# Rounding a weight transfer's two halves with one instruction

## The chip, the cores and the metric

One core of a Trainium2 chip runs the program. The metric is device microseconds of one execution, as the median of several runs. The engines named below are PE (TensorE: the matmuls, with PEld for the loads of their stationary operand), ACT (ScalarE), DVE (VectorE), POOL (GpSimd) and SP (which issues the weight transfers).

## What is computed

Two blocks run on 256 tokens of width 1024 (plus 16 meta tokens in the first block). Cut to what matters here:

```
first block:   h = rms_norm(stream);  proj = h @ w_in
               y_a = layer_norm(depthwise_conv(a * sigmoid(gate))) -> silu -> @ conv_pw_out
               y_b = top-k sparse attention -> @ attn_w_o
               stream += (g_a * y_a + g_b * y_b) @ w_merge_out
               stream += (silu(a) * b_) @ ffn_down,   a, b_ = depthwise_conv(h @ ffn_up)
               out = rms_norm(stream)
second block:  layer 0: gated linear attention (GLA), layer 1: block attention (MoBA);
               after each:  x = layer_norm(alpha * x + y)
                            x = layer_norm(alpha * x + (silu(gate) * up) @ w_down)
```

All of it is float32, and each weight is used for all tokens once it has arrived.

## The kernel before

**How a product is made.** Each float32 factor is split into a high part (the value rounded to the type fp32r) and a rest (value minus high part, again fp32r), and a product is three matmuls: high times high, high times rest, rest times high. `mm_ws` (L173) has the weights as the stationary operand, `mm_xs` (L179) has them as the moving one. Activations are split by `split` (L199): an ACT copy for the high part, a DVE subtraction for the rest.

**How weights arrive.** The host packs all weights, in their order of use, into 167 chunks of 128 x 2048 (1 MB). `emit_raw` (L112) issues one transfer for each chunk from SP into a ring of three `wraw` tiles. A chunk is two halves of 1024 columns, and a half is the unit of use: `next_half` (L164) hands out the next one. In a projection (`proj_tile`, L188) a half is the stationary operand of 24 matmuls; in the down projections (L741) and in `xs_cols` (L868) it is the moving operand of 512 columns.

**How weights are split.** `emit_split` (L122) emits, for each half, an ACT copy into `whi` (L134) and a DVE subtraction into `wlo` (L136). Each of the two has a ring of LOOK + 1 = 6 tiles of 1024 columns. `may_split` (L144) sets how far ahead of use this goes: with half h about to be used, halves up to h + 5 are emitted. The tile of half h + 5 is that of half h - 1, so that its ACT copy waits until PE has finished the last matmul of half h - 1. `hold` (L156) puts a limit on this ahead of a normalization, `go_on` (L159) lifts it. Twelve "early" halves (L80) go to tiles of their own.

**What sets the order.** Each engine runs its instructions in one order that is fixed when the program is built. A planner makes it from the order in which the program emits them, their dependences and its own estimate of when each can start: an instruction that it holds to be ready goes ahead of an earlier one that isn't. Only inside `manual_schedule` blocks (the first normalization, L702, L772, `norms` L844) do DVE and ACT keep the order of the program.

**The stages, by the start of the span.** Convolution, index scores and sparse attention of the first block run until about 200 us, the merge until 274 us, the first feed-forward until 466 us, GLA until 586 us, the second feed-forward until 773 us, MoBA until 885 us, the third feed-forward until the end. A feed-forward (`ffn`, L710) goes through its 22 hidden tiles in groups of two: four halves of up projections (two for each hidden tile, with the results in `pa` and `pb`), then two halves of down projections. For each hidden tile `evac2` (L934; `evac1`, L756, in the first feed-forward) makes the activation `g_`, and `split` (L730) turns it into `rg_h` and `rg_l`, the stationary operands of the down projections. A group of four opens the second and third feed-forward, a group of six (TAIL) closes each.

Of the kernel before, what the change touches and what calls it, by code (L numbers as in the profile page):

```python
# [10 lines left out]
F32R = mybir.dt.float32r  # L11
# [5 lines left out]
P = 128  # L17
# [17 lines left out]
HALF = 1024  # L35
CHUNK = 2 * HALF
# [44 lines left out]
EARLY_SET = {e + i for e in EARLY for i in range(4)}  # L81
# [3 lines left out]
def tile_hybrid(ctx: ExitStack, tc: tile.TileContext, x, meta, wts, misc, vec, cst, rows, gkw, ng, pos,  # L85
# [5 lines left out]
    wp = ctx.enter_context(tc.tile_pool(name="wp", bufs=1))  # L91
# [14 lines left out]
    LOOK = LK  # L106
    RAW_BUFS = 3
    raws, halves = {}, {}
    state = {"raw": 0, "split": 0, "use": 0, "cap": 2 * N_CHUNKS, "early": None}
    early = []  # L110

    def emit_raw(upto):  # L112
        while state["raw"] < min(upto, N_CHUNKS):
            c = state["raw"]
            t = wp.tile([P, CHUNK], F32, name="wraw", tag="wraw", bufs=RAW_BUFS)
            for a in range(0, CHUNK, HALF if c == 0 else CHUNK):
                b = a + (HALF if c == 0 else CHUNK)
                nc.sync.dma_start(t[:, a:b], wts[c, :, a:b])
            raws[c] = t
            state["raw"] += 1  # L120

    def emit_split(upto, later=None):  # L122
        while state["split"] < min(upto, 2 * N_CHUNKS):
            h = state["split"]
            emit_raw(h // 2 + 1)
            r = raws[h // 2][:, (h % 2) * HALF:(h % 2 + 1) * HALF]
            if h in EARLY_SET:
                hi, lo = state["early"](len(early) % 4)
                early.append((hi, lo))
            else:  # L130
                hi = wp.tile([P, HALF], F32R, name="whi", tag="whi", bufs=LOOK + 1)
                lo = wp.tile([P, HALF], F32R, name="wlo", tag="wlo", bufs=LOOK + 1)
                halves[h] = (hi, lo)
            A.activation(hi, r, AF.Copy)  # L134
            if later is None:
                V.tensor_sub(lo, r, hi.bitcast(F32))  # L136
            else:
                later.append(lambda r=r, hi=hi, lo=lo: V.tensor_sub(lo, r, hi.bitcast(F32)))
            state["split"] += 1
            if h % 2 == 1:  # L140
                del raws[h // 2]
                emit_raw(h // 2 + RAW_BUFS)

    def may_split(h):  # L144
        n = state["split"]
        if n >= 2 * N_CHUNKS:
            return False
        if n <= h:
            return True
        if n >= state["cap"]:  # L150
            return False
        if n in EARLY_SET and state["early"] is None:
            return False
        return sum(i not in EARLY_SET for i in range(h, n)) <= LOOK

    def hold(n):  # L156
        state["cap"] = state["use"] + n
# [1 line left out]
    def go_on(n=None):  # L159
        state["cap"] = 2 * N_CHUNKS if n is None else state["cap"] + n  # L160
        while may_split(state["use"]):
            emit_split(state["split"] + 1)

    def next_half():  # L164
        h = state["use"]
        while may_split(h):
            emit_split(state["split"] + 1)
        state["use"] += 1
        while state["use"] in EARLY_SET:
            state["use"] += 1  # L170
        return halves.pop(h)
# [56 lines left out]
    def rsqrt(r, v, mul, eps):  # L228
        if mul != 1.0:
            V.tensor_scalar(v, v, mul, eps, op0=OP.mult, op1=OP.add)  # L230
        else:
            V.tensor_scalar(v, v, eps, None, op0=OP.add)
        nc.gpsimd.tensor_tensor(r, v, mhalf[:r.shape[0], :r.shape[-1]], op=OP.pow)
        return r
# [62 lines left out]
    with tc.high_priority(), tc.manual_schedule(engines={ENG.PE, ENG.DVE, ENG.Activation}):  # L297
# [24 lines left out]
        later = []  # L322
        A.activation(rw[:, META:], pr[:, META:], AF.Copy)
        emit_split(1, later)
        hs = {}

# [445 lines left out]
    with tc.high_priority(), tc.manual_schedule(engines={ENG.DVE, ENG.Activation}):  # L772
        for t in range(2):
# [5 lines left out]
            r = rsqrt(st[:, 3:4], st[:, 2:3], 1.0 / D, EPS)  # L779
            lo = []  # L780
# [209 lines left out]
    with tc.manual_schedule(engines={ENG.Activation}):  # L990
        for t in range(2):
            pz = ps_wk()
            PE.matmul(pz, gkT[:, t * P:(t + 1) * P], gw, start=True, stop=True)
            z = bp.tile([P, D], F32, name="z", tag="y", bufs=2)[:, :512]
# [66 lines left out]
    for g in range(2):  # L1061
        for t in range(2):
            with tc.high_priority():
                po2 = ps_wk()
                st = sc.tile([P, 2, 2], F32, name="st4", tag="st4", bufs=2)
                for a in range(2):
                    h = 2 * g + a
# [6 lines left out]
                r = rsqrt(st[:, :, 1], st[:, :, 0], 1.0 / 256, EPS)  # L1074
                for a in range(2):
                    h = 2 * g + a
# [242 lines left out]
```

## Time and profile before

| what | value |
|---|---|
| median of three runs | 1074.8 us |
| lowest and highest | 1074.72 and 1075.06 us |
| the profiled execution | 1076.28 us |
| its span in the trace | 1074.5 us |
| its mean granted TensorE clock | 0.995 of full speed |
| busy: PE, PEld, DVE, ACT, POOL | 1054.8, 954.5, 739.5, 601.0, 44.1 us |
| read from HBM | 183.96 MB, 172 GB/s over the span |

The span is the profiled execution from the first to the last record on the core; 1.78 us of that execution lie around it. The busy time of an engine is the time in which at least one of its instructions runs. Matmuls overlap, so that the duration of one is longer than the distance between the starts of two; where the pace of PE matters, the distance between starts is the number to take.

### The profile page before, as it was taken

The numbers are of one execution on the slowest core, as the hardware profiler recorded it, in microseconds if no ns is written. First come the engines' busy times: TensorE is split into PE (matmuls) and PEld (weight loads), VectorE is DVE, ScalarE is ACT, GpSimd is POOL, SyncE is SP. The second block draws the span as 40 slices with busy tenths as digits, with TensorE's granted clock in tenths as the row PEclk, the third lists the DMA queues.
The fourth block names the chain that finished last, engine by engine and source line by source line (L and its number), as shares of the span: only waits on it lengthen the run. The fifth ranks groups of instructions, "written<-read, shape, count | busy, mean of one in ns | idle before, by whom it ended". The sixth has DMA issues, their size and how long they took to land. (4 is left out here: it accounts for less than half of the span.)

```text
span 1074.5 us, 17515 instructions
## 1 busy us (share of the span) xinstructions
PE 1054.8 (98%) x6989; PEld 954.5 (89%) x6989; DVE 739.5 (69%) x1291; ACT 601.0 (56%) x1051; POOL 44.1 (4%) x52
## 2 busy tenths in 40 slices
PE   8999999999999999999999999999999999999997
PEld 8998998899899999977877999999888878999995
DVE  6899999995776767774577655556674766555555
ACT  6897698564555555567463444446256925444440
POOL 0131002100000000000000000000000000000000
PEclk8999999999999999999999999999999999999999
DMA  8886556564354555454453655557263436555541
GB/s 307 246 201 161 191 166 178 148 220 169 142 197 160 195 182 192 174 185 139 153 202 112 236 196 179 180 191 274 79 215 138 164 131 226 187 195 194 173 144 40
DMA packets 33333, 192.37 MB, mean 179 GB/s; under 512 B 3889, under 2 KB 7857, under 8 KB 12002
## 3 DMA queue, kind: packets, MB, share of 16 engines
q1 hardware_dynamic: 28002, 185.02, 49.7%
q0 software_dynamic: 5248, 6.23, 3.6%
q8 instruction: 55, 0.90, 0.3%
q14 instruction: 28, 0.23, 0.1%
HBM read 183.96 MB, written 1.05 MB: 172 GB/s over the span
## 5 line engine op out<-in xcount | busy, mean ns | idle before, releaser
L136 DVE TENSOR_TENSOR wlo<-wraw,whi 128x1024 fp32r<-128x1024 f32 x320 | 388.5, 1223 | 204.8 <-ACT whi L134 203.9
L134 ACT ACTIVATE whi<-wraw 128x1024 fp32r<-128x1024 f32 x322 | 337.3, 1058 | 302.0 <-PE ps_wk L176 117.7
L176 PE MATMUL ps_wk<-hT_l,whi 128*128 128x256 f32 (+1 forms) x976 | 274.9, 282 | 0.0
L177 PE MATMUL ps_wk<-hT_h,wlo 128*128 128x256 f32 (+1 forms) x976 | 274.6, 281 | 0.0
L175 PE MATMUL ps_wk<-hT_h,whi 128*128 128x256 f32 (+1 forms) x976 | 274.2, 281 | 0.0
L175 PEld LDWEIGHTS ps_wk<-hT_h,whi 128*128 128x128 f32 x976 | 184.4, 189 | 1.1
L176 PEld LDWEIGHTS ps_wk<-hT_l,whi 128*128 128x128 f32 x976 | 184.0, 189 | 1.4
L177 PEld LDWEIGHTS ps_wk<-hT_h,wlo 128*128 128x128 f32 x976 | 184.8, 189 | 0.4
L181 PE MATMUL ps_acc<-whi,rg_h 128*128 128x512 f32 x328 | 131.1, 400 | 0.0
L182 PE MATMUL ps_acc<-wlo,rg_h 128*128 128x512 f32 x328 | 129.6, 395 | 0.0
L183 PE MATMUL ps_acc<-whi,rg_l 128*128 128x512 f32 x328 | 127.1, 395 | 0.0
L175 PE MATMUL ps_acc<-hT_h,whi 128*128 128x258 f32 (+2 forms) x352 | 101.9, 290 | 0.0
L177 PE MATMUL ps_acc<-hT_h,wlo 128*128 128x258 f32 (+2 forms) x352 | 100.7, 286 | 0.0
L176 PE MATMUL ps_acc<-hT_l,whi 128*128 128x258 f32 (+2 forms) x352 | 100.5, 285 | 0.0
L183 PEld LDWEIGHTS ps_acc<-whi,rg_l 128*128 128x128 f32 x328 | 61.6, 188 | 14.7 <-DVE rg_l L202 0.2
L181 PEld LDWEIGHTS ps_acc<-whi,rg_h 128*128 128x128 f32 x328 | 61.6, 188 | 14.1 <-ACT rg_h L200 0.2
L182 PEld LDWEIGHTS ps_acc<-wlo,rg_h 128*128 128x128 f32 x328 | 61.7, 188 | 12.8
L181 PE MATMUL ps_acc<-whi,hT_h 128*128 128x512 f32 (+1 forms) x184 | 71.8, 390 | 0.0
L183 PE MATMUL ps_acc<-whi,hT_l 128*128 128x512 f32 (+1 forms) x184 | 70.8, 385 | 0.0
L182 PE MATMUL ps_acc<-wlo,hT_h 128*128 128x512 f32 (+1 forms) x184 | 70.6, 384 | 0.0
L175 PEld LDWEIGHTS ps_acc<-hT_h,whi 128*128 128x128 f32 x352 | 66.2, 188 | 0.3
L176 PEld LDWEIGHTS ps_acc<-hT_l,whi 128*128 128x128 f32 x352 | 66.3, 188 | 0.2
(950 smaller groups left out, 1561.7 us busy)
## 6 DMA issues: line engine op xcount, KB each, us to landing
wraw<-in_wts_dram SPq DMA_DIRECT2D x166, 1024.0 KB, 5.0
ysum<-zs POOLq DMA_DIRECT2D x10, 258.0 KB, 6.9
x<-in_x_dram SPq DMA_DIRECT2D x4, 512.0 KB, 3.8
lg<-in_rows_dram SPq DMA_DIRECT2D x4, 512.0 KB, 3.6
lb<-in_rows_dram SPq DMA_DIRECT2D x4, 512.0 KB, 5.4
wraw<-in_wts_dram SPq DMA_DIRECT2D x2, 512.0 KB, 6.5
out_dram<-x SPq DMA_DIRECT2D x4, 256.0 KB, 2.0
mraw<-in_misc_dram SPq DMA_DIRECT2D x1, 576.0 KB, 12.3
```

Of the source, the lines that this page charges most:

```text
L134: A.activation(hi, r, AF.Copy)
L136: V.tensor_sub(lo, r, hi.bitcast(F32))
L175: PE.matmul(ps, wh, xh, start=first, stop=False)
L176: PE.matmul(ps, wh, xl, start=False, stop=False)
L177: PE.matmul(ps, wl, xh, start=False, stop=last)
L181: PE.matmul(ps, xh, wh, start=first, stop=False)
L182: PE.matmul(ps, xh, wl, start=False, stop=False)
L183: PE.matmul(ps, xl, wh, start=False, stop=last)
```

## The change

The two halves of a chunk share one tile of 2048 columns in each of the rings `whi` and `wlo`, which now have three tiles. One ACT instruction rounds both halves and one DVE instruction makes both rests (n = 2). The first chunk keeps one instruction for each half, and so do the early halves. `may_split` counts pairs: a pair is emitted when no more than two pairs, that of the half in use among them, lie between the use and it. The use of a half, the transfers and all matmuls stay as they are.

```diff
@@ emit_split
             h = state["split"]
             emit_raw(h // 2 + 1)
-            r = raws[h // 2][:, (h % 2) * HALF:(h % 2 + 1) * HALF]
+            n = 1 if h in EARLY_SET or h < 2 else 2
+            r = raws[h // 2][:, (h % 2) * HALF:(h % 2 + n) * HALF]
             if h in EARLY_SET:
                 hi, lo = state["early"](len(early) % 4)
                 early.append((hi, lo))
             else:
-                hi = wp.tile([P, HALF], F32R, name="whi", tag="whi", bufs=LOOK + 1)
-                lo = wp.tile([P, HALF], F32R, name="wlo", tag="wlo", bufs=LOOK + 1)
-                halves[h] = (hi, lo)
+                if h % 2 == 0:
+                    both = [wp.tile([P, CHUNK], F32R, name=nm, tag=nm, bufs=(LOOK + 1) // 2) for nm in ("whi", "wlo")]
+                    for i in range(2):
+                        halves[h + i] = tuple(z[:, i * HALF:(i + 1) * HALF] for z in both)
+                hi, lo = both if n == 2 else halves[h]
             A.activation(hi, r, AF.Copy)
...
-            state["split"] += 1
-            if h % 2 == 1:
+            state["split"] += n
+            if state["split"] % 2 == 0:
                 del raws[h // 2]
                 emit_raw(h // 2 + RAW_BUFS)
@@ may_split
-        return sum(i not in EARLY_SET for i in range(h, n)) <= LOOK
+        return len({i // 2 for i in range(h, n) if i not in EARLY_SET}) <= LOOK // 2
```

## Rows read from the trace of the kernel before

**Rows 1.** The page of the profile: busy time of each engine with its share of the span and its instructions.
```profile
PE 1054.8 (98%) x6989; PEld 954.5 (89%) x6989; DVE 739.5 (69%) x1291; ACT 601.0 (56%) x1051; POOL 44.1 (4%) x52
```

**Rows 2.** Busy time of each engine in stretches of the span. Columns: the stretch, its length, busy us (and instructions) of PE, PEld, DVE, ACT, POOL, granted clock, DMA share, GB/s.
```profile
100.00:200.00 100.00, 99.10 (x758) 91.64 (x758) 98.46 (x254) 77.99 (x195) 13.14 (x14) 1.00 0.59 161
...
490.00:520.00 30.00, 30.00 (x131) 24.35 (x130) 14.21 (x14) 16.68 (x19) 0.00 (x0) 1.00 0.40 140
...
640.00:700.00 60.00, 60.00 (x416) 55.66 (x415) 31.60 (x37) 26.29 (x35) 0.00 (x0) 1.00 0.54 187
```

**Rows 3.** Waits of PE over the whole span: who waited for whom, us in total, times, the longest.
```profile
PE ps_wk L638 <- POOL rs L635: 1.9, 2, 1.4
PE ps_wk L474 <- ACT r L477: 1.8, 2, 1.6
...
PE ps_acc L176 <- DVE sT_l L202: 0.5, 1, 0.5
PE ps_wk L648 <- DVE sqb L646: 0.4, 1, 0.4
```

**Rows 4.** The page's costliest groups: the two that the change touches. Columns: count, busy us and mean ns of one, idle time of the engine just before them and what ended most of it.
```profile
L136 DVE TENSOR_TENSOR wlo<-wraw,whi 128x1024 fp32r<-128x1024 f32 x320 | 388.5, 1223 | 204.8 <-ACT whi L134 203.9
L134 ACT ACTIVATE whi<-wraw 128x1024 fp32r<-128x1024 f32 x322 | 337.3, 1058 | 302.0 <-PE ps_wk L176 117.7
```

**Rows 5.** Timeline of ACT, then of DVE, at the end of a group's up projections in the second feed-forward (start us, us, engine and line, idle time before it and its releaser).
```profile
711.38 1.06 ACT L134 ACTIVATE whi<-wraw 128x1024 fp32r<-128x1024 f32 x1 [1.52 <-PE ps_wk L176]
712.35 0.40 ACT L200 ACTIVATE rg_h<-g__7765 128x256 fp32r<-128x256 f32 x1
...
711.52 0.42 DVE L937 TENSOR_TENSOR g__7765<-g__7765,ps_wk 128x256 f32<-128x256 f32 x1 [0.67 <-PE ps_wk L177]
712.48 1.23 DVE L136 TENSOR_TENSOR wlo<-wraw,whi 128x1024 fp32r<-128x1024 f32 x1 [0.54 <-ACT whi L134]
713.62 0.42 DVE L202 TENSOR_TENSOR rg_l<-g__7765,rg_h 128x256 fp32r<-128x256 f32 x1
```

**Rows 6.** Timeline of PE at the same place: the last matmul of the up projections, the first of the group's first down projection, and the first three of its second.
```profile
711.13 0.28 PE L177 MATMUL ps_wk<-hT_h,wlo 128*128 128x256 f32 x1
711.25 0.40 PE L181 MATMUL ps_acc<-whi,rg_h 128*128 128x512 f32 x1
...
714.04 0.40 PE L181 MATMUL ps_acc<-whi,rg_h 128*128 128x512 f32 x1
714.27 0.40 PE L182 MATMUL ps_acc<-wlo,rg_h 128*128 128x512 f32 x1
714.50 0.40 PE L183 MATMUL ps_acc<-whi,rg_l 128*128 128x512 f32 x1
```

**Rows 7.** Timeline of PE, then one row of DVE, at the same place of a group in the first feed-forward: the end of the first down projection, the first and last of 13 matmuls after it, and the second down projection.
```profile
323.50 0.39 PE L183 MATMUL ps_acc<-whi,rg_l 128*128 128x512 f32 x1
323.73 0.28 PE L175 MATMUL ps_wk<-hT_h,whi 128*128 128x258 f32 x1
...
325.16 0.28 PE L175 MATMUL ps_wk<-hT_h,whi 128*128 128x258 f32 x1
325.35 0.51 PE L181 MATMUL ps_acc<-whi,rg_h 128*128 128x512 f32 x1
...
326.85 0.86 PE L183 MATMUL ps_acc<-whi,rg_l 128*128 128x512 f32 x3
...
326.16 0.42 DVE L202 TENSOR_TENSOR rg_l<-g__4080,rg_h 128x256 fp32r<-128x256 f32 x1
```

**Rows 8.** Timeline at the start of GLA, where freshly split halves are the next that PE needs: ACT, DVE, then PE (xN: a run of N instructions with its whole length).
```profile
462.43 3.91 ACT L134 ACTIVATE whi<-wraw 128x1024 fp32r<-128x1024 f32 x4 [1.71 <-PE ps_acc L183]
...
463.52 4.63 DVE L136 TENSOR_TENSOR wlo<-wraw,whi 128x1024 fp32r<-128x1024 f32 x4 [2.08 <-ACT whi L134]
468.07 0.15 DVE L778 TENSOR_TENSOR st<-st 128x1 f32<-128x1 f32 x1
...
465.70 0.39 PE L900 MATMUL ps_acc<-whi,hT_h 128*128 128x512 f32 x1
465.93 0.39 PE L901 MATMUL ps_acc<-wlo,hT_h 128*128 128x512 f32 x1
...
469.98 0.63 PE L245 MATMUL ps_wk<-cs,x 128*128 128x128 f32 x4 [0.44 <-DVE x L784]
...
472.75 0.39 PE L900 MATMUL ps_acc<-whi,hT_h 128*128 128x512 f32 x1
```

**Rows 9.** Timeline where `go_on` lifts a limit after a normalization: six high parts and six rests in one run, and PE's first matmul with the first of those rests, in the second feed-forward (586 to 593 us). Then two rows from the start of the program: a run of four high parts, and PE's first matmul with the first of their rests.
```profile
587.11 5.80 ACT L134 ACTIVATE whi<-wraw 128x1024 fp32r<-128x1024 f32 x6
...
588.22 6.90 DVE L136 TENSOR_TENSOR wlo<-wraw,whi 128x1024 fp32r<-128x1024 f32 x6
...
592.43 0.28 PE L177 MATMUL ps_wk<-hT_h,wlo 128*128 128x256 f32 x1
...
18.16 3.89 ACT L134 ACTIVATE whi<-wraw 128x1024 fp32r<-128x1024 f32 x4
...
22.73 0.29 PE L177 MATMUL ps_acc<-hT_h,wlo 128*128 128x272 f32 x1
```

**Rows 10.** DVE's groups of instructions in the stretch from 25 to 203 us.
```profile
L136 DVE TENSOR_TENSOR wlo<-wraw,whi 128x1024 fp32r<-128x1024 f32 x48 | 58.4, 1219 | 3.0 <-ACT whi L134 2.9
```

**Rows 11.** The page's DMA issues: the weight transfers. Columns: count, KB each, us from issue to landing (median).
```profile
wraw<-in_wts_dram SPq DMA_DIRECT2D x166, 1024.0 KB, 5.0
```

## The prediction

> **What bounds the kernel now.** I read the busy times first [rows 1]: PE is busy for 1054.8 of 1074.5 us, while DVE and ACT, the two engines that the change relieves, are busy for 739.5 and 601.0. An average hides stages, so the table by stretches came next [rows 2]. In the feed-forwards PE has no idle time at all (60.00 of 60), DVE works half of the time. In the first block, from 100 to 200 us, DVE is as full as PE (98.46 against 99.10 of 100). So DVE's load can matter in the first block and nowhere else. Then I asked what PE waits for [rows 3]: the waits shown are 1.9, 1.8, 0.5 and 0.4 us, and none is on a weight. The whole wait of ACT ahead of its 322 roundings, 302.0 us, ends mostly with PE giving a tile free [rows 4]: ACT waits for PE, not the other way round. The change has little to win, then, and the question is where a coarser step makes something late.
>
> **The price of a pair.** A rounding of 1024 columns takes 1058 ns [rows 4], one of 256 columns 0.40 us [rows 5]: 0.857 ns for a column, so 1.94 us for 2048. A rest takes 1223 ns for 1024 and 0.42 us for 256: 1.046 ns for a column, so 2.29 us. No row has 2048 columns; the bounds are one half (1.06 and 1.22 us) and two halves (2.12 and 2.45 us). I take 1.94 and 2.29, since both come from rows of the same operation. In a run of six the starts stand (5.80 - 1.06) / 5 = 0.95 us apart on ACT and (6.90 - 1.22) / 5 = 1.14 us on DVE [rows 9], so an end overlaps the next start by 0.11 and 0.09 us. A pair then saves 2 x 0.95 - (1.94 - 0.11) = 0.07 us of ACT and about as much of DVE. For 160 pairs that is some 11 us on each, nearly all of it beside PE's work: counted at nothing, with PE's matmuls as the cover.
>
> **What comes later, in steady state.** Before, half h + 5 was rounded when half h - 1 was done. Now its pair is rounded when the older pair is done, at that same moment if h + 5 is odd, one half later (2.8 us) for the first half of the pair. The rounding ends 0.88 us later and the rest 0.88 + 1.07 = 1.95 us later. A half is needed at the earliest four halves after its pair is emitted, over 11 us, against 1.94 + 2.29 = 4.23: covered. The tile of a transfer comes free 1.95 us later and SP issues the next one that much later. It takes 5.0 us [rows 11] and is needed two chunks later, again some 11 us: covered. No queue is crossed; no transfer is added.
>
> **The feed-forward groups.** This is the tightest place in the trace. The up projections of a group end at 711.25 [rows 6]. ACT's rounding at 711.38 goes ahead of `rg_h`, and DVE's rest ahead of `rg_l`, which ends at 713.62 + 0.42 = 714.04 [rows 5]. PE wants it for the matmul at 714.50, its load 0.2 us ahead. With a pair at this place the rounding ends at 713.32, `rg_h` at about 713.6 (wanted at 714.04: in time), the pair's rest runs until 715.6 and `rg_l` ends at 715.95: 1.45 us late. Whether this costs anything depends on PE's order. In the first feed-forward `rg_l` is late by more than that today, and there [rows 7] the order of PE has 13 matmuls of the next up projection and then six with `rg_h` ahead of the first with `rg_l`. The planner had foreseen the delay and put other work into it. With a pair it can do the same in the second and third: eight matmuls with `rg_h` at 0.233 us are 1.87 us, which reaches from 714.04 to 715.90. I count 0 for the 20 groups (8 in the first feed-forward, 6 in each of the others). The bounds are 0 and 20 x 0.1 = 2.0 us, if the planner is off by 0.1 each time.
>
> **The start of GLA.** Here no cover is large enough. Four roundings run from 462.43, as the last chain of the down projections lets go of one tile every 0.70 us; the four rests run until 468.15; the normalization's step at 468.07 stands behind them, and PE waits 0.44 us for it at 469.98 [rows 8]. Now the first pair can't begin before its second old half is done: 462.43 + 0.70 = 463.13, rounded at 465.07, its rest at 467.36. The second pair is rounded at 466.9, its rest at 469.56. So DVE's step comes 1.4 us later, at 469.5, and the transposes at 471.4. PE wants a rest at 465.93. In the best order it does eight matmuls with high parts and eight with rests, the last four from 469.56 to 470.5 instead of ending at 469.4, 1.1 us late. Then the transposes' wait of 0.44 is filled by the eight matmuls that came after them, and the next token tile starts at about 473.2 instead of 472.75. That is +0.45. In the order of today it is +1.05. I take +0.5, nearer to the row of today in which the planner fills gaps.
>
> **The other starts.** In the second feed-forward the first rest is due now at 587.11 + 1.94 + 2.29 = 591.34 and is wanted at 592.43, less 0.2 for its load; at the start of the program it is due at 18.16 + 4.23 = 22.39 and is wanted at 22.73 less 0.2 [rows 9]. Both are covered: 0, bounds 0 and 0.3 for the tighter one. Without the cover, each microsecond would be one of the total.
>
> **The first block.** DVE is full there, and 48 rests are recorded between 25 and 203 us [rows 10]: 24 pairs x 0.07 = 1.7 us less work. At most that comes off the waits of PE at L638, L648 and L176, the convolution's normalization. Against it, a step of a chain that falls behind a pair waits up to 1.07 us longer. Bounds -1.7 and +1.1, taken at -0.3, because those waits [rows 3] hang on chains in which POOL and ACT take part as well.
>
> **The sum.** +0.5 - 0.3 + 0 = +0.2 us. The profiled execution took 1076.28 us, 1.48 more than the median, with 1.78 us of it around the span; the difference carries over to either. From the median: 1075.0 us.
>
> **A rule that says otherwise.** PE's load row is busy for 954.5 us, 89%, and from 490 to 520 us for 24.35 of 30 [rows 1, 2]. The Trainium skill ("Perfetto Trace Analysis", Identifying the Most-Contended Engine) holds that the busy time of matmuls is no good measure of how close PE is to its limit and that the share of weight loads is a better one. By that PE would have a tenth to spare, and freeing ACT and DVE could pay. Here the starts of matmuls stand 0.23 us apart with nothing waited for [rows 6], so I don't believe in that tenth; it is the first rival.
>
> **The rivals.**
> *Faster: PE is fed better.* What freed engines could take away are waits of PE that end with DVE, ACT or POOL: 1.9 + 1.8 + 0.5 + 0.4 = 4.6 us [rows 3]: 1070.2 us. For it speaks the full DVE of the first block. Against it, 0.07 us a pair is too little to move those chains. Chance 0.09.
> *Slower: a rest of the activations stuck behind a pair.* If PE's order of today stays, the late `rg_l` is a wait. The place is the third matmul of a group's second down projection, the price 1.45 us in 12 groups and 1.95 in the 8 of the first feed-forward: 17 + 16 = 33 us, 1108 us. It decides from the point at which the planner expects `rg_l` before PE reaches it. For it: the slack today is a quarter of a microsecond [rows 5, 6]. Against it: the order in rows 7 shows what the planner does with a late operand. Chance 0.08, with part of it (a few tenths a group) between 1079 and 1090.
> *Slower by less: longer steps in dense chains.* In the first block and in attention every chain step queues behind whatever DVE runs. If three of the waits in rows 3 grow by 1.07 us each, +3.2 beside the +0.2: about 1078. Chance 0.17.
> *The pair costs two halves.* Nothing is saved; at GLA both runs end some 0.3 us later: 1075.5. Chance 0.05, inside "no change".
> *The forecast,* 1075.0, its own range 1073.5 to 1076.9: 0.61.
>
> **How the numbers follow.** About 0.2% (2.1 us) is what a measurement of this kernel can tell from no change: below 1072.65 is faster, above 1076.95 slower. Faster: 0.09. Slower: 0.08 and 0.14 of the 0.17, together 0.22. No change: 0.69. The bounds of the unknown costs alone give 1074.8 + 0.45 - 1.7 = 1073.5 and 1074.8 + 1.05 + 2.0 + 0.3 + 1.1 = 1079.3. The range reaches a little into the faster rival and holds the third: 1072.3 to 1079.6. It leaves out most of the faster rival and the stall, some 0.15.
>
> **What would show it.** Right: 160 fewer instructions in each of the two groups; durations near 1.94 and 2.29 us; PE idle nowhere in the feed-forwards, with L181 and L182 in a run ahead of L183 in the second down projection of a group, as in rows 7; a rest at GLA's start that ends near 469.5, and PE some half a microsecond later behind it. Wrong: waits of PE on `rg_l` or `wlo` in the feed-forwards; gaps of PE near 87, 214 or 221 us that grow or vanish; a pair far from 1.94 and 2.29 us.

## The result

The changed kernel takes 1090.2 us (median of 5 runs, 1088.8 to 1091.6) against 1074.8 of the kernel before: a ratio of 1.0143, 95% interval 1.0128 to 1.0158. It is slower by 15.4 us, where no change was forecast. Its profiled execution took 1091.62 us with a span of 1089.8.

Beside the experiments the kernel before gave medians of 1074.9 to 1077.5, so each is compared by its ratio to the runs of it that were made with it. Runs of one kernel differ with TensorE's mean granted clock as well (e17 below: 1079.15 us at 0.996, 1085.4 at 0.991), so stages are read from the profiled executions.

Line numbers of the changed kernel are higher by 3 from the rounding on: L137 is the rounding, L139 the rest, L178 to L180 and L184 to L186 are the matmuls.

### The profile page after: what moved, and what is told of

It is laid out like the page before. It is cut to its first block, busy times and chain, and to the rows that moved or that the text cites. A ratio compares the mean times of both kernels' runs of the same rounds, so it can differ in the third digit from the quotient of the medians.

```text
span 1089.8 us, 17084 instructions
## 1 busy us (share of the span) xinstructions
PE 1063.5 (98%) x6989; PEld 958.7 (88%) x6989; DVE 716.9 (66%) x1131; ACT 580.0 (53%) x891; POOL 43.3 (4%) x52
## 3 DMA queue, kind: packets, MB, share of 16 engines
HBM read 183.96 MB, written 1.05 MB: 170 GB/s over the span
## 5 line engine op out<-in xcount | busy, mean ns | idle before, releaser
L139 DVE TENSOR_TENSOR wlo<-wraw,whi 128x2048 fp32r<-128x2048 f32 x160 | 365.0, 2289 | 227.4 <-ACT whi L137 227.1
L137 ACT ACTIVATE whi<-wraw 128x2048 fp32r<-128x2048 f32 (+1 forms) x162 | 306.7, 1903 | 253.0 <-PE ps_wk L179 111.7
L180 PE MATMUL ps_wk<-hT_h,wlo 128*128 128x256 f32 (+1 forms) x976 | 274.6, 281 | 0.0
L178 PE MATMUL ps_wk<-hT_h,whi 128*128 128x256 f32 (+1 forms) x976 | 274.2, 281 | 0.0
L180 PEld LDWEIGHTS ps_wk<-hT_h,wlo 128*128 128x128 f32 x976 | 184.7, 189 | 1.5
L178 PEld LDWEIGHTS ps_wk<-hT_h,whi 128*128 128x128 f32 x976 | 184.4, 189 | 1.4
L184 PE MATMUL ps_acc<-whi,rg_h 128*128 128x512 f32 x328 | 130.7, 402 | 0.5
L186 PE MATMUL ps_acc<-whi,rg_l 128*128 128x512 f32 x328 | 121.1, 399 | 0.1
L178 PE MATMUL ps_acc<-hT_h,whi 128*128 128x258 f32 (+2 forms) x352 | 102.0, 290 | 0.0
L180 PE MATMUL ps_acc<-hT_h,wlo 128*128 128x258 f32 (+2 forms) x352 | 100.3, 286 | 0.0
L184 PEld LDWEIGHTS ps_acc<-whi,rg_h 128*128 128x128 f32 x328 | 61.6, 188 | 15.9 <-ACT rg_h L203 2.4
L186 PEld LDWEIGHTS ps_acc<-whi,rg_l 128*128 128x128 f32 x328 | 60.1, 188 | 14.3 <-DVE rg_l L205 0.4
L184 PE MATMUL ps_acc<-whi,hT_h 128*128 128x512 f32 (+1 forms) x184 | 71.8, 390 | 0.0
L186 PE MATMUL ps_acc<-whi,hT_l 128*128 128x512 f32 (+1 forms) x184 | 71.4, 388 | 0.0
L178 PEld LDWEIGHTS ps_acc<-hT_h,whi 128*128 128x128 f32 x352 | 66.3, 188 | 0.4 <-ACT th L367 0.2
```

The costliest lines, as they stand in the source:

```text
L178: PE.matmul(ps, wh, xh, start=first, stop=False)
L180: PE.matmul(ps, wl, xh, start=False, stop=last)
L184: PE.matmul(ps, xh, wh, start=first, stop=False)
L186: PE.matmul(ps, xl, wh, start=False, stop=last)
```

## The profile after

The page's first line, beside [rows 1]:

```profile
PE 1063.5 (98%) x6989; PEld 958.7 (88%) x6989; DVE 716.9 (66%) x1131; ACT 580.0 (53%) x891; POOL 43.3 (4%) x52
```

ACT and DVE were relieved by some 21 and 23 us, as meant. PE has the same 6989 matmuls, is busy 8.7 us longer, and idle for 26.3 us in place of 19.7. The page's groups, beside [rows 4], show 160 instructions fewer each, and the price of a pair:

```profile
L139 DVE TENSOR_TENSOR wlo<-wraw,whi 128x2048 fp32r<-128x2048 f32 x160 | 365.0, 2289 | 227.4 <-ACT whi L137 227.1
L137 ACT ACTIVATE whi<-wraw 128x2048 fp32r<-128x2048 f32 (+1 forms) x162 | 306.7, 1903 | 253.0 <-PE ps_wk L179 111.7
```

What PE waits for, beside [rows 3] (engine, line, who released it: us in total, times, longest):

```profile
PE ps_acc L178 <- ACT sT_h L203: 4.7, 1, 4.7
PE ps_wk L651 <- DVE sqb L649: 2.9, 1, 2.9
...
PE ps_acc L904 <- DVE wlo L139: 1.3, 1, 1.3
...
PE ps_wk L641 <- POOL rs L638: 1.0, 2, 0.5
PE ps_wk L477 <- ACT r L480: 0.7, 2, 0.5
```

Two waits in the convolution's normalization have grown (0.4 to 2.9 us on `sqb`, 0.5 on `sT_l` to 4.7 on `sT_h`), and one on a weight is new (GLA's start). Some have shrunk: on `r` by 1.1 us, on `rs` by 0.9. Where the time went is read by landmarks, the start of the same event in both traces: the second transposes of a row of `rs` (L638, now L641; the merge's normalization), the first transposes of `x` behind the first feed-forward, and the first ahead of the second feed-forward (L245, now L248).

| stage | before | after | more |
|---|---|---|---|
| A: to the merge's normalization | 273.13 | 281.07 | 7.9 |
| B: first feed-forward, to 458.55 / 470.79 | 185.42 | 189.72 | 4.3 |
| C: GLA, to 577.64 / 592.28 | 119.09 | 121.49 | 2.4 |
| D: the rest, with two feed-forwards | 496.86 | 497.52 | 0.7 |

Stage A. The windows of 5 us of the changed kernel, here and at the start of stage B (busy times with instructions; the third number from the right is PE's granted clock):

```profile
200.00:205.00 5.00, 2.13 (x18) 1.92 (x16) 5.00 (x7) 0.96 (x1) 0.00 (x0) 0.93 0.62 167
205.00:210.00 5.00, 5.00 (x28) 4.62 (x29) 3.90 (x7) 2.80 (x5) 0.00 (x0) 0.73 0.67 236
...
220.00:225.00 5.00, 1.27 (x11) 1.06 (x9) 5.00 (x12) 3.73 (x4) 0.00 (x0) 0.98 0.67 231
225.00:230.00 5.00, 4.08 (x18) 3.93 (x19) 3.04 (x8) 5.00 (x14) 0.00 (x0) 0.50 0.58 206
230.00:235.00 5.00, 5.00 (x37) 5.00 (x37) 2.20 (x6) 1.67 (x5) 0.00 (x0) 0.84 0.35 110
...
280.00:285.00 5.00, 3.91 (x22) 3.25 (x21) 3.40 (x11) 2.80 (x8) 0.85 (x1) 0.78 0.03 10
285.00:290.00 5.00, 5.00 (x39) 5.00 (x39) 4.82 (x9) 2.17 (x2) 0.00 (x0) 0.88 0.00 0
```

PE runs dry twice, and the clock is down behind each of the waits. Before, it was 1.00 in all these windows, as in this one:

```profile
225.00:230.00 5.00, 5.00 (x45) 5.00 (x43) 5.00 (x9) 2.72 (x4) 0.00 (x0) 1.00 0.94 312
```

The wait near 221 us, by the timeline of ACT after (start, duration, and in brackets the idle time ahead and who ended it):

```profile
213.25 1.92 ACT L137 ACTIVATE whi<-wraw 128x2048 fp32r<-128x2048 f32 x1 [0.93 <-PE ps_acc L179]
215.08 0.40 ACT L655 ACTIVATE sqb<-yc 128x258 f32<-128x258 f32 x1
221.24 1.91 ACT L137 ACTIVATE whi<-wraw 128x2048 fp32r<-128x2048 f32 x1 [5.76 <-issue]
223.17 1.28 ACT L662 ACT_TABLE_LOAD   x1
224.46 1.09 ACT L662 ACTIVATE yc<-yc,vecs 128x258 f32<-128x258 f32 x2
225.46 0.71 ACT L203 ACTIVATE sT_h<-yc 128x258 fp32r<-128x258 f32 x2
```

and before:

```profile
211.63 1.06 ACT L134 ACTIVATE whi<-wraw 128x1024 fp32r<-128x1024 f32 x1 [1.50 <-PE ps_acc L176]
212.72 1.28 ACT L659 ACT_TABLE_LOAD   x1
216.75 1.10 ACT L659 ACTIVATE yc<-yc,vecs 128x258 f32<-128x258 f32 x2 [2.75 <-DVE yc L658]
217.75 0.71 ACT L200 ACTIVATE sT_h<-yc 128x258 fp32r<-128x258 f32 x2
```

The rounding at 221.24 starts when PE ends its last matmul with `oT` (220.99 + 0.28). It is that of halves 60 and 61, whose tile is free only then. Four other halves come ahead of them in the projections of `sT`, some 11 us of PE's work. The silu's input was there at about 220.55. Behind the rounding it waits 0.7 us for PE, 1.91 for the pair and 1.28 for the table load, which before was done long ahead. So PE waits for ACT, and ACT has waited for PE.

The wait near 202 us, by DVE:

```profile
199.22 1.23 DVE L426 TENSOR_TENSOR yc<-yc,ysum 128x1032 f32<-128x1032 f32 x1 [3.19 <-DMA ysum<-zs]
200.37 2.28 DVE L139 TENSOR_TENSOR wlo<-wraw,whi 128x2048 fp32r<-128x2048 f32 x1
202.57 1.29 DVE L648 TENSOR_TENSOR sqb<-yc 128x516 f32<-128x516 f32 x2
...
204.12 0.69 DVE L649 TENSOR_TENSOR sqb<-sqb 128x516 f32<-128x516 f32 x1
```

A pair's rest stands between the last partial sum and the sums that PE waits for, 1.06 us more than a half's, and the last partial sum itself (L426), which waits for its transfer, comes 0.63 us later than before (198.59). PE reaches the place 0.77 us earlier (202.00 for 202.77). That makes the 2.46 us by which this wait grew.

Stage B. In each of eight groups PE gets `rg_h` late: the matmul below starts 0.34 us behind the one ahead of it, where matmuls of 258 columns stand 0.12 us apart. PE's rows, then ACT's:

```profile
337.67 0.28 PE L179 MATMUL ps_wk<-hT_l,whi 128*128 128x258 f32 x1
338.01 0.51 PE L184 MATMUL ps_acc<-whi,rg_h 128*128 128x512 f32 x1
...
331.05 1.92 ACT L137 ACTIVATE whi<-wraw 128x2048 fp32r<-128x2048 f32 x1 [2.13 <-PE ps_wk L179]
...
337.09 0.56 ACT L754 ACTIVATE a__3985<-ps_wk,vecs 128x256 f32<-128x256 f32 x1 [3.06 <-PE ps_wk L180]
337.56 0.41 ACT L203 ACTIVATE rg_h<-g__3894 128x256 fp32r<-128x256 f32 x1
```

Groups stand 17.58 us apart (the waits recur at 320.43, 338.01 and 355.60), 17.21 before (308.14, 325.35, 342.57). The pair's rounding (331.05 to 332.97) goes ahead of L754 on ACT, its rest (333.00 to 335.29) ahead of L756 on DVE, `g` is ready at 337.07 and `rg_h` at 337.97. The last step of this is the planner's: with `g` there, ACT still takes the next hidden tile's L754 first (337.09), 0.47 us, which it does not do at this place before. Eight groups at 0.37 us are 3.0. The low clock from 280 to 290 us is the other part, by an estimate from the last two of those windows: 0.22 x 3.91 + 0.12 x 5.00 = 1.5 us. The kernels of the table below bear it out: with long roundings in B, they lose 2.8 to 3.0 us there where the clock stays at 1.00 from 275 to 290 us (e5, e10, e16), and 4.0 to 4.3 where it falls.

Stage C, around the first rest, beside [rows 8]; the timelines of ACT, DVE and PE:

```profile
475.36 3.72 ACT L137 ACTIVATE whi<-wraw 128x2048 fp32r<-128x2048 f32 x2 [2.41 <-PE ps_acc L186]
477.31 4.49 DVE L139 TENSOR_TENSOR wlo<-wraw,whi 128x2048 fp32r<-128x2048 f32 x2 [3.64 <-ACT whi L137]
477.94 0.40 PE L903 MATMUL ps_acc<-whi,hT_h 128*128 128x512 f32 x1
479.66 0.50 PE L904 MATMUL ps_acc<-wlo,hT_h 128*128 128x512 f32 x1 [1.33 <-DVE wlo L139]
...
486.63 0.40 PE L903 MATMUL ps_acc<-whi,hT_h 128*128 128x512 f32 x1
```

The first rounding starts when the last old half is done, its rest ends 4.2 us later, and PE has one matmul with a high part to fill the time, not eight. The next token tile starts at 486.63, 15.84 us behind the landmark at 470.79; before, it was 14.20 (472.75 behind 458.55). So 1.6 of the 2.4 us are lost here.

## The experiments

The theory (A) was that long instructions, which wait for two old halves, stand ahead of chains that PE waits for. Rivals: the planner's new order as such (B), and the feed-forwards (C). These letters of the theories are not those of the stages. The ratios are of medians; the last four columns are the stages' differences from the kernel before in us, each in one profiled execution:

| kernel | ratio, 95% interval | A | B | C | D |
|---|---|---|---|---|---|
| changed kernel | 1.0143 (1.0128 to 1.0158) | 7.9 | 4.3 | 2.4 | 0.7 |
| e2, short instructions, pair tiles | 1.0058 (1.0043 to 1.0073) | 1.5 | 2.2 | 1.8 | 0.4 |
| e5, short in the first block | 1.0056 (1.0037 to 1.0075) | 1.5 | 3.0 | 2.5 | 0.6 |
| e6, rounding pair only | 1.0118 (1.0101 to 1.0134) | 6.4 | 4.0 | 1.8 | 1.1 |
| e7, rest pair only | 1.0074 (1.0048 to 1.0099) | 3.0 | 0.6 | 2.7 | -0.3 |
| e8, one pair behind the silus | 1.0098 (1.0075 to 1.0121) | 4.7 | 4.3 | 2.4 | 0.6 |
| e10, two pairs moved | 1.0091 (1.0076 to 1.0107) | 3.9 | 2.8 | 2.5 | 0.3 |
| e11, and short in B | 1.0105 (1.0088 to 1.0122) | 7.6 | 1.1 | 1.8 | 1.0 |
| e12, before in a new order | 1.0038 (1.0024 to 1.0051) | 1.4 | 1.4 | 0.1 | 0.1 |
| e13, filler in time | 1.0125 (1.0104 to 1.0146) | 6.7 | 4.2 | 2.4 | 0.7 |
| e14, after in a new order | 1.0100 (1.0075 to 1.0126) | 5.2 | 4.2 | 2.4 | 0.8 |
| e15, before in a third order | 0.9999 (0.9981 to 1.0017) | -1.6 | 0.0 | 0.2 | -0.3 |
| e16, after in a third order | 1.0134 (1.0113 to 1.0156) | 8.9 | 2.8 | 2.4 | 0.4 |
| e17, two places mended | 1.0082 (1.0055 to 1.0109) | -1.0 | 0.6 | 2.7 | 0.5 |

**Short instructions in the pair tiles (e2), only later pairs (e5).** Of the condition for a pair, e2 leaves none, and e5 those behind the first block:

```
-            n = 1 if h in EARLY_SET or h < 2 else 2
+            n = 1                                        # e2
+            n = 1 if h in EARLY_SET or h < 72 else 2     # e5
```

> The tiles of 2048 columns stay, handed round by pairs, but each half is rounded, and its rest made, by an instruction of its own. The instructions are short again, the release is coarse. If the coarse release alone makes the loss (one form of theory A): 1085 to 1091 us, with the long wait of PE near 221 us still there. If the length of the instructions does it (the other form): 1075 to 1078 us. Rival B (order): anything from 1076 to 1091, with its waits at places other than those of the changed kernel. Rival C: 1075 to 1078 if length counts there, 1079 if release does.

1081.9 us in e2: neither form. The length of the instructions loses 8.5 thousandths; tile pairs and their order lose 5.8. The wait near 221 us is gone, that near 202 us is 0.17. What is left lies at the merge's normalization (A's end and B's start, with a clock of 0.52 from 275 to 280 us) and in C.

> In the tiles of 2048 columns, single instructions for the 72 halves that are used ahead of the first feed-forward, pairs for all later ones. Theory A now says: what the length of the instructions loses in the convolution's normalization (some 10 us with the low clock behind it, 198 to 260 us) is gone, as it is with short instructions everywhere (0.3 us there); what pairs lose in the first feed-forward (2.7 us) and at the start of GLA (1.5) stays, and so may the 4 us that short instructions lose around 271 to 285 us: 1079 to 1084 us. Rival C (the feed-forwards carry it): 1086 to 1090. Rival B (order): no bound, and the loss at places that neither of the other kernels has.

1083.7 us in e5, within what theory A gave: A falls to 1.5, C keeps its loss, and B what it loses at full clock.

**One engine's pairs (e6, e7).** In e6 the rest, in e7 the rounding is issued by halves:

```
-                V.tensor_sub(lo, r, hi.bitcast(F32))             # e6
+                for i in range(n):
+                    s_ = slice(i * HALF, (i + 1) * HALF)
+                    V.tensor_sub(lo[:, s_], r[:, s_], hi[:, s_].bitcast(F32))
...
-            A.activation(hi, r, AF.Copy)                         # e7
+            for i in range(n):
+                s_ = slice(i * HALF, (i + 1) * HALF)
+                A.activation(hi[:, s_], r[:, s_], AF.Copy)
```

> ACT rounds a pair by one instruction, DVE makes the two rests by two. Theory A says that it is ACT's pair ahead of the table load and the silus that makes the long wait of PE near 221 us, and ACT's pair ahead of the activations' rounding that stretches the groups of the first feed-forward: 1086 to 1091 us, with the wait near 221 us over 3 us and a first feed-forward 2 to 3 us longer than before. If DVE's long rests are what blocks: 1079 to 1083. Rival B: not bound.

> The reverse: ACT rounds half by half, DVE makes both rests by one instruction. Theory A (ACT's pair): 1079 to 1084 us, the first feed-forward as before, the wait near 221 us under 2 us; the wait near 202 us, which hangs on DVE, may stay at 2 to 3 us. If DVE's long rests are what blocks: 1086 to 1091.

1089.0 us in e6 and 1083.3 in e7, both as theory A has it. With the rounding in pairs the wait on `sT_h` is there in full and B loses 4.0; with only the rest in pairs PE does not wait for `sT_h` at all, and B loses 0.6. The waits of PE in e6:

```profile
PE ps_acc L180 <- ACT sT_h L205: 4.6, 1, 4.6
PE ps_wk L653 <- DVE sqb L651: 3.0, 1, 3.0
```

and in e7:

```profile
PE ps_wk L643 <- POOL rs L640: 2.9, 2, 2.3
...
PE ps_wk L653 <- DVE sqb L651: 2.0, 1, 2.0
PE ps_acc L906 <- DVE wlo L141: 1.4, 1, 1.4
```

So it is ACT's pair that costs at `sT_h` and in B. The long rest has a smaller part in A, and 0.6 to 0.9 us of C (2.4 to 2.7 in the kernels with long rests there, 1.8 in the three without, e2, e6 and e11).

**One pair moved (e8).** A dependency that only orders binds the rounding of halves 60 and 61 behind the last rounding of `sT`:

```
+            if h in (60, 61):
+                tc.add_manual_dep(rounding.ins, behind[-1].ins.name, LATER, reason="behind")
```

> The changed kernel with one pair of 160 moved: the rounding that stood on ACT at 221.24 us, ahead of the table load and the silus (halves 60 and 61, wanted some 11 us later), is bound behind the last rounding of the silus' results. Theory A: the silus start near 220.6 instead of 224.46, the wait of 4.65 us shrinks to under 1.2, and the low clock behind it (0.50 and 0.84 in the two stretches of 5 us after it, some 2.8 us) goes with it: 1082 to 1085 us. If the clock does not hang on that wait: 1086 to 1087. Rival B (the order as a whole): 1088 to 1092. Rival C: 1090.

1086.9 us, outside the 1082 to 1085 of theory A and inside what was said for a clock that does not hang on this wait. The stages tell the two apart: the wait of 4.65 is now 0.7 + 0.7, and the clock from 225 to 235 us is 1.00, but the wait near 202 us grew to 3.7, with 0.50 behind it from 205 to 210. The waits of PE in e8:

```profile
PE ps_wk L654 <- DVE sqb L652: 3.7, 1, 3.7
...
PE ps_acc L181 <- ACT sT_h L666: 0.7, 1, 0.7
PE ps_acc L181 <- DVE tg L671: 0.7, 1, 0.7
```

One instruction of 160, moved, makes stage A 3.2 us shorter.

**Two pairs moved (e10), and short instructions in B (e11).** e10 also binds the rest of halves 52 and 53 behind L649; e11 has short instructions in B on top:

```
+                if h in (52, 53):
+                    tc.add_manual_dep(rest.ins, behind[0].ins.name, LATER, reason="behind")
...
+            n = 1 if h in EARLY_SET or h < 2 or 72 <= h < 180 else 2     # e11
```

> The changed kernel with two places of 160 pairs mended: the rounding of halves 60 and 61 behind the silus, as in the run before, and the rest of halves 52 and 53, which stood on DVE at 200.37 us ahead of the sums that PE waits for at 202 us, behind those sums. Theory A: the wait near 202 us (2.86 in the changed kernel, 3.65 with the one pair moved) falls under 1.5, the wait near 221 us stays under 1.5, and the clock of 0.50 to 0.73 from 205 to 210 us rises to over 0.9: 1081 to 1084.5 us. If these two places are not what loses the 10 us ahead of 240 us: 1086 or more. Rival B (order): not bound, new waits elsewhere.

> As the last, and with single instructions for halves 72 to 179 (the first feed-forward and the start of GLA; the tiles stay pairs). Theory A, stage by stage: less 2.8 us of the first feed-forward, perhaps half a microsecond at the start of GLA: 1077.5 to 1081.5 us, with one short wait ahead of the activations in a group of the first feed-forward, as before, in place of two. Rival C would have it under 1077. Rival B (order): 1082 or more with a new wait.

Both missed: 1085.5 us in e10 and 1087.1 in e11. In e10 the sums are ready 1.94 us earlier (202.92 for 204.86), but PE reaches the place 2.25 us earlier too (199.75 for 202.00), since the planner puts it earlier in PE's order: the wait stays 3.2. In e11, B falls to 1.1, as expected, while A loses 3.6 more than in e10 by longer waits (3.8 us near 202 us for 3.2, and 2.9 in all from 277 to 282 for 1.1). A mend in one place gave the planner another order in the next. That gave rival B its weight.

**The planner's order (e12, e15 before; e14, e16 after).** Edits that leave the work as it is:

```
-            for a in range(0, CHUNK, HALF if c == 0 else CHUNK):
+            for a in range(0, CHUNK, CHUNK):                            # e12, e14
+            for a in range(0, CHUNK, HALF if c < 4 else CHUNK):         # e15
...
-WIX = 1
+WIX = 3                                                                 # e16
```

> A control for rival B on the kernel before: its first chunk of weights comes by one transfer in place of two. Nothing else is touched, but the planner's order comes out anew (71 rows of PE, 125 of ACT and 169 of DVE stand elsewhere). Theory A: the first weights come up to 2 us later, and that hides in part behind the normalization: 1074 to 1077.5 us. Rival B (any new order costs several microseconds): 1079 or more, lost behind 30 us.

> The kernel before with its first four chunks by two transfers each; 69 rows of PE, 140 of ACT and 196 of DVE stand elsewhere, and it is another order than that of the other control. Theory A: 1074 to 1081 us, with no wait of PE over 2.5 us behind 30 us. Rival B: 1074 to 1092.

> The changed kernel with its first chunk by one transfer, which did to the kernel before what is told of it: a new order, 3.9 us more. Here 94 rows of PE, 141 of ACT and 214 of DVE stand elsewhere. Theory A (long steps ahead of chains and in the groups of the first feed-forward, whatever the order): 1086 to 1096 us. Rival B (the order alone): it may come out anywhere from 1076 to 1095, under 1082 as likely as over 1090.

> The changed kernel with the eight index weights transposed behind the fourth projection of q in place of the second; 63 rows of PE, 67 of ACT and 127 of DVE stand elsewhere. Theory A: 1084 to 1094 us, with the first feed-forward 2.5 to 3 us longer than before the change and a wait of over 1 us at the start of GLA in every order. Rival B: 1076 to 1094.

Three orders of the kernel before give 1.000, 1.0038 and 0.9999, three of the changed one 1.0143, 1.0100 and 1.0134. With 1079.3 us, e12 came out as rival B had it and above theory A's 1077.5; e15, e14 and e16 (1075.3, 1088.9 and 1091.5) lie in theory A's ranges, and in B's wide ones too. The two groups of three do not meet, so order alone is not the cause; it is worth some 4 us. What moves with it is the wait near 202 us (0.3 in e14, 3.7 in e16). What does not move is the wait on `sT_h`. In e14:

```profile
PE ps_acc L178 <- ACT sT_h L203: 4.7, 1, 4.7
```

in e16:

```profile
PE ps_acc L178 <- ACT sT_h L203: 4.8, 2, 4.7
```

Nor do 2.8 us in B where the clock stays at 1.00 (e16), and 2.4 in C.

**Filler for the low clock (e9, e13).** Matmuls of no use in front of the projections of `sT`:

```
+    pf = ps_wk()
+    for _ in range(8):
+        filler = PE.matmul(pf[:, :NQ], ident, tg[0][:, 0, :], start=True, stop=True)
+        tc.add_manual_dep(filler.ins, final[-1].ins.name, LATER, reason="behind")
```

> The changed kernel with ten matmuls of no use (identity by a finished tile of tg, 258 columns, float32, into a work bank that nobody reads), placed behind the projections of oT, where PE sits idle for 4.65 us. They keep PE at work until sT is there and take nothing else away. If it is the idle time that lowers the clock behind it (0.50 from 225 to 230 us, 0.84 from 230 to 235): granted 1.00 there, 2.5 to 3 us less: 1087 to 1088.5 us. If the low clock has another cause: 1090 to 1092, since the filler itself may end some tenths of a microsecond late. Rival B (order): no rows of ACT or DVE move, so as the latter.

> The changed kernel with eight matmuls of no use whose operand is there long before, bound behind the last projection of oT in PE's order; no row of ACT or DVE moves. They fill some 4 us of the 4.65 that PE sat idle near 221 us and end before sT is there. If idleness lowers the clock: granted 1.00 from 225 to 240 us (0.50 and 0.84 in the changed kernel), 2.5 to 3 us less: 1086.5 to 1088.5 us. If the clock falls for another cause: 1089.5 to 1091.5.

In e9 (1090.9 us, 1.0140) the operand was late, PE was idle for 2.1 us all the same, and the filler put the first matmul with `sT` off to 230.30, over 3 us behind its operand: this settles nothing. In e13 the filler ran in time and the clock held (the same windows as above):

```profile
225.00:230.00 5.00, 3.81 (x22) 3.00 (x23) 2.62 (x8) 5.00 (x14) 0.00 (x0) 1.00 0.60 210
230.00:235.00 5.00, 5.00 (x44) 5.00 (x43) 2.89 (x7) 2.51 (x4) 0.00 (x0) 1.00 0.34 108
```

Still it takes 1090.7 us, which is what was said for another cause of the low clock (1.0125, an interval that meets that of the changed kernel). Yet with the filler the clock did hold, so it is the price of the low clock that was set too high, not the cause that was wrong. From the first matmul with `sT` to the end of stage A it takes 54.31 us in place of 55.15: 0.8 gained, not 2.5 to 3. At full clock PE waits for the silus (1.7 us in three waits on `sT_h`), which come by pairs every 1.6 us. The low clock there lay mostly in their shadow.

**Both places mended (e17)**, in the order of e14: e8's dependency, and for `72 <= h < 166` two roundings of 1024 in place of one.

> The changed kernel in the order of its first control (first chunk by one transfer, 1088.9 us there), with the rounding of halves 60 and 61 bound behind the silus and with ACT rounding half by half for halves 72 to 165, the first feed-forward; the rests and all else stay pairs. If these two places lose what they seem to: 3.3 and 2.8 us less, and up to 1.5 more where the clock stays at 1.00 behind the merge: 1081.5 to 1084 us, the wait near 218 us under 1.5 and no wait on rg_h over 0.1 us a group. If a new order eats it: 1086 or more.

1083.6 us, in the expected range. In the profiled execution (a span of 1077.3 us, e14's is 1087.1) A is 1.0 us shorter than before the change and B 0.6 longer: both losses are gone in it. It is the fastest of the four, 4.4 us below the median; where the others lose more is not known. The times alone do not show the gain: the interval, 1.0055 to 1.0109, meets e14's. What the trace does show is that the waits are gone. PE's longest behind the start, in e17:

```profile
PE ps_acc L913 <- DVE wlo L147: 1.4, 1, 1.4
PE ps_wk L485 <- ACT r L488: 1.4, 1, 1.4
```

On `sT_h` it waits 0.5 us. Left are the 2.7 us of C, 0.5 of D, and a run-to-run spread (1079.2 to 1086.5) that goes with the granted clock (0.996 to 0.991).

**One tile fewer, before the change (e18).**

```
-LK = 5
+LK = 4
```

> The kernel before with five tiles of 1024 columns in place of six: every half is rounded one half later than before, as the first half of a pair is after the change; no instruction is longer, no tile is a pair. If the late release is what loses at the start of GLA (1.8 us between the two norms that bound it, 126.3 us before, with short instructions in pair tiles): 1 to 2 us there, none in the groups of the first feed-forward, 1076.5 to 1080 us in all. If it is the pair as such: that stretch stays at 126.3 to 126.8 us, 1074.5 to 1077 in all.

1088.2 us (1.0119, 1.0102 to 1.0136). B and C together lose 1.3 us, as expected of a late release, and nothing of it between 280 and 440 us, in B's groups. The total missed both ranges by far: A loses 2.4 us, and D 8.5, where no kernel of the table loses more than 1.1. In D the normalization behind the second feed-forward became a wait:

```profile
774.46 1.32 PE L245 MATMUL ps_wk<-cs,x 128*128 128x128 f32 x8 [2.67 <-DVE x L823]
```

Before, these transposes start at 763.50, among the last down projections; here they stand behind all of them. In the same way the program ends 12.2 us behind PE's last matmul, in place of 7.7. So a late release costs at the start of GLA without any pair, in the one order that was timed; what it costs in D lies at places where the changed kernel loses nothing, and comes with another order.

**A ring (e1, e3, e4).** Slices of one standing tile in place of tiles handed round, with singles, pairs behind half 72, and pairs up to it:

```
+    RING = [wp.tile([P, (LK + 1) * HALF], F32R, name=nm) for nm in ("whi", "wlo")]
...
+                hi, lo = (z[:, q * HALF:(q + n) * HALF] for z in RING)
```

> A control. The rounding and the rest are made half by half as before the change, but into slices of one standing tile of six halves in place of six tiles that are handed round. Nothing that the change speaks of is in it; only the planner's picture of who waits for whom differs, so that its order comes out anew (some 370 rows of PE's order differ). Theory A (a pair's long instruction, which waits for two old halves, stands ahead of the convolution's normalization on ACT and DVE, PE runs dry there and its clock falls): 1074 to 1077 us, no wait of PE over 1.5 us between 198 and 230 us. Rival B (any new order costs, the order of before was a lucky one): 1080 us or more, with a wait of PE somewhere that before did not have. Rival C (pairs cost in the feed-forwards): as A.

> Singles for the 72 halves that are used ahead of the first feed-forward, pairs for all later ones, both in slices of one standing tile. Theory A: what is lost from 198 to 230 us with its low clock, some 10 us of the 15.4, is gone; what the first feed-forward (about 2.7) and the start of GLA (1.4) lose stays: 1078 to 1081 us. Rival C (the feed-forwards): 1086 to 1090. Rival B: not told by the place, 1078 to 1090.

> The other way round: pairs for the 72 halves ahead of the first feed-forward, singles for all later ones. Theory A: 1083 to 1087 us, with the waits of PE near 202 and 221 us and a granted clock under 0.9 in the 15 us behind them. Rival C: 1075 to 1079. Rival B: anything between.

1100.2 us in e1, 1112.1 in e3 and 1112.9 in e4, which say nothing of the change. A group takes several halves before it writes its matmuls; in a ring a slice is then overwritten, in program order, ahead of the matmuls that should read it, so that these compute with a later half and wait for it.

## Why the prediction was wrong

**The price of a pair** was right: 1.91 and 2.29 us (1.94 and 2.29 said). What a pair saves was not: 0.07 us on each engine was said, 11 us in all, and it is 21 us of ACT and 23 of DVE, 0.13 and 0.14 a pair. The steady state was right: D, with two feed-forwards, loses 0.7 us.

**The first block** is the step that failed: "a step of a chain that falls behind a pair waits up to 1.07 us longer", bounds -1.7 and +1.1, taken at -0.3. It measured +7.9 (stage A). I priced the longer instruction and not its place in a queue. A pair that waits for both old halves stands ahead of the chain until PE is through with them, and holds the table load behind it: 3.9 us for the silus at one place. I had looked at `rg_l` in this way, and not at the silus, though the place of my third rival (three waits, 1.07 each) was the right one, and so was the sign that I named for being wrong, a gap near 221 us that grows: from 0.5 to 4.65. For the wait on `sT_h` this is shown by e7 and e8, and borne out by e17's trace. The wait near 202 us is the order's in part (none over 0.15 us in e17, 3.9 in e9); what sets it in each is not settled.

**The feed-forward groups**, counted at 0 with bounds 0 and 2.0, took about 2.8 in the first feed-forward, and some 1.5 of low clock at its start. What I feared, `rg_l` behind the pair's rest, was filled by the planner, as said; what was late is `rg_h`, which I had put in time, by the pair's rounding ahead of L754. e6 and e7 show it to be ACT's long instruction. How much of the 0.37 us a group is the length and how much the next tile's L754 ahead of `rg_h` was not taken apart.

**The start of GLA**, +0.5 with bounds 0.45 and 1.05, took 1.6 at its place and 2.4 in the stage: the mechanism was right, the size was off. ACT and DVE did as worked out: counted from the first transposes (458.55 and 470.79), the second rest was to end after 11.01 us and ended after 11.01. PE did not: it kept its order of high parts and rests in turn, so that it waited 1.33 us for the first rest. Later in the stage a wait of 0.6 on `gs` (0.2 before) came on top; the rest of the difference is not accounted for. Of the 2.4, 1.8 is there with short instructions as well (e2). What e2 shares with the changed kernel is the tile that is released by pairs, and the new order.

**The other starts** cost nothing, as said. **PE fed better**, the first rival, was priced at 4.6 us from four of PE's waits; all that the trace shows sum to 11.4, 3.8 of them at the start of the program. Two did shrink, on `r` (1.8 to 0.7 us) and on `rs` (1.9 to 1.0), by the freed engines or by the new order, which is not shown. The rule weighed there, the Trainium skill's on the share of weight loads ("Perfetto Trace Analysis", Identifying the Most-Contended Engine), is not borne out here: with loads at 89% of the span before and 88% after, 21 us less of ACT and 23 less of DVE made none of the four stages shorter.

## What to carry to other kernels

When instructions are merged, look at where the merged one will stand in its engine's queue and whom it waits for there; its longer duration is the small part. A prefetch that waits for a buffer must not stand ahead of a chain which the buffer's reader waits for. And where a planner orders the work, time a neutral change of order first: here it is worth some 4 us, and a smaller gain can't be told from a new order by the time alone.

## What the hardware showed

PE's granted clock fell to 0.50 (1.2 of 2.4 GHz) for 5 us behind a wait of 4.65 us. Behind shorter waits it is not the same from kernel to kernel: 0.66 from 215 to 220 us behind one of 1.28 us (e5), 1.00 there behind one of 1.28 us as well (e15) and behind one of 1.39 (before). Behind the same two waits of 0.54 and 0.55 us at the merge's normalization it was 1.00 in some profiled executions (before, e15, e16, e17) and 0.66 to 0.78 in a stretch of 5 us just behind them in others (after, e12, e14); some 1.4 us of stage B come and go with it. And a low clock costs little where PE would have waited anyway: in e13 a clock held at 1.00 gained 0.8 us.
